# Low parts of every second down-projection block by a negated copy and an accumulating DMA

## The chip, the core and the metric

One core of a Trainium2 chip. Its engines work beside each other and meet at semaphores: PE (TensorE, matrix products), DVE (VectorE), ACT (ScalarE), POOL (GpSimd), and SP (SyncE), which here only issues DMAs. Each engine takes its instructions in the order of the program. The metric is the device time of one execution in microseconds (us), the median of several runs. The profile comes from one execution of its own.

## The reference

A decoder trunk of two layers over 256 tokens of width 1024. Each layer has three sub-layers: a SwiGLU with inner width 2816, a mixer (a gated recurrence, a state-space block and a gated token mixing, between two projections), and another SwiGLU. Around each stands a norm before and one after.

```
def swiglu(x, w_gu, w_down):
    g, u = jnp.split(x @ w_gu, 2, axis=-1)
    return (jax.nn.silu(g) * u) @ w_down

for l in range(DEPTH):
    f = swiglu(rms_norm(x, ffn1_pre_g[l]), ffn1_w_gu[l], ffn1_w_down[l])
    x = x + 0.5 * rms_norm(f, ffn1_post_g[l])
    m = hybrid_mixer(rms_norm(x, mix_pre_g[l]), mix_w_in[l], mix_w_out[l], ...)
    x = x + rms_norm(m, mix_post_g[l])
    f = swiglu(rms_norm(x, ffn2_pre_g[l]), ffn2_w_gu[l], ffn2_w_down[l])
    x = x + 0.5 * rms_norm(f, ffn2_post_g[l])
```

Everything is float32. The kernel reaches that precision with a faster product type (fp32r) by splitting each operand in a high part, its rounding to fp32r, and a low part, what the rounding left; three products (high by high, high by low, low by high) replace one.

## The kernel before

**Weights.** All weights stream through the core once, in the order of use, as blocks of 128 rows by 512 columns (some are narrower). Four blocks make a chunk. SyncE loads chunk after chunk (L345) into three staging buffers `stg` in turn, so chunk n + 3 goes into the buffer of chunk n as soon as all four blocks of chunk n have been read. A block is then split into a slot: a tile with a high half `hi` and a low half `lo`. There are 17 slots `s_w`, and a few spare ones (`s_a`) may be lent from another pool during a down projection. A slot comes free when PE has done the last product with its block. So weights are split ahead of PE as far as free slots reach.

**The split** (`split_next`, L383 to L404). Blocks that carry a norm's gain are scaled on the way (L400 on ScalarE, L401 on VectorE). Down-projection blocks carry none: ScalarE casts staging to the high half (L396), VectorE subtracts it from the staging for the low half (L397):

```
if not sc:
    self.keep(nc.scalar.copy(hi, src))
    self.keep(nc.vector.tensor_tensor(out=lo, in0=src, in1=hi.bitcast(F32), op=ALU.subtract))
```

**A SwiGLU** has six stages of gate and up products (L704), whose results go through silu, product and split on ScalarE and VectorE, and then the down projection (`down`, L738): 22 rows of two blocks, each block multiplied for two token tiles of 128, three products each (`mm3`, L425). The last four rows are done first for token tile 0 and then for token tile 1, so that the norm of tile 0 (`post`, L533) runs beside the products of tile 1. In `post`, ScalarE squares and sums each half of the result (tile `junk`), VectorE multiplies by the gain (`s_f`), POOL takes the power -1/2 (`postr`), VectorE makes the new x, and PE transposes it for the next sub-layer (`pre`, L569). These transposes stand in PE's order inside the products of tile 1.

**Order.** Python code issues side computations by planned times, and a scheduler then places the instructions of each engine. The result is one fixed list for each engine.

Of the kernel before, what the change touches and what calls it, by code (L numbers as in the profile page):

```python
# [8 lines left out]
F32 = mybir.dt.float32  # L9
F32R = mybir.dt.float32r  # L10
BF16 = mybir.dt.bfloat16
AF = mybir.ActivationFunctionType
# [3 lines left out]
P = 128  # L16
# [91 lines left out]


class Chain:  # L110
    """A side computation: a generator whose operations are issued when their inputs are due."""

    def __init__(self, k, t=None):
        self.k = k
# [107 lines left out]
class Kernel:  # L222
# [35 lines left out]
        self.wt, self.wh, self.wready, self.slot_time = {}, {}, {}, {}  # L258
        self.extra, self.keep_free = 0, 4

    # ---------------------------------------------------------------- memory
    def get(self, shape, dtype=F32, kind="a"):
        tag = self.free_slots[kind].pop(0)
        return self.scr.tile(shape, dtype, tag=tag, name="s_" + tag), (kind, tag)
# [24 lines left out]
        o, w = BCOL[name]  # L289
        return self.pb[:, o:o + w]  # L290

    # ---------------------------------------------------------------- issue order
    def keep(self, ins, pin=False):
        if pin or self.now() < PIN:
            self.tc.keep_in_program_order(ins)
# [39 lines left out]
    def drain(self):  # L335
        self.wait_for(lambda: not self.chains)

    # ---------------------------------------------------------------- weights
    def dma_chunk(self):
        ci = self.next_dma  # L340
        self.next_dma += 1
# [41 lines left out]
    def split_next(self, kind):  # L383
        d = self.next_split
        nc, T = self.nc, self.T
        u = self.units[d]
        w = unit_width(u)
        ci, o = self.u2c[d]
        src = self.ctile[ci][:, o:o + w]
        t, h = self.get([P, 2, 512], F32R, kind)  # L390
        hi, lo = t[:, 0, :w], t[:, 1, :w]
        sc = u[3] is not None
        T["act"] = max(T["act"], self.carrive[ci], self.slot_time.get(h, 0.0) + HOP) + 0.095 + w * 0.000833 + 0.095 * sc
        T["dve"] = max(T["dve"], T["act"] + HOP) + 0.07 + 0.06 * sc + w * 0.00104
        if not sc:
            self.keep(nc.scalar.copy(hi, src))  # L396
            self.keep(nc.vector.tensor_tensor(out=lo, in0=src, in1=hi.bitcast(F32), op=ALU.subtract))  # L397
        else:
            s = self.pcol(u[1], u[3][0], u[3][1])
            self.keep(nc.scalar.activation(hi, src, AF.Copy, scale=s))  # L400
            self.keep(nc.vector.scalar_tensor_tensor(out=lo, in0=src, scalar=s, in1=hi.bitcast(F32),  # L401
                                                     op0=ALU.mult, op1=ALU.subtract))
        self.wt[d], self.wh[d], self.wready[d] = t, h, T["dve"]
        self.next_split += 1  # L404
# [11 lines left out]
        self.slot_time[h] = self.now()  # L416
        self.put(h)

    # ---------------------------------------------------------------- main products
    def mm3(self, out, st, mv, start, stop):  # L420
        (sh, sl), (mh, ml) = st, mv
        mm = self.nc.tensor.matmul
# [11 lines left out]
        st = tuple(self.nT[:, i, k, t * P:(t + 1) * P] for i in range(2))  # L434
        self.mm3(bk[0][:, :w], st, (wt[:, 0, :w], wt[:, 1, :w]), start, stop)

    # ---------------------------------------------------------------- setup
    def setup(self):
        nc, cp = self.nc, self.cp
        self.cur = 0  # L440
# [21 lines left out]
        self.T["pool"] = 2.0  # L462

    def softplus(self, c, out, x, n, tag):
        """out = softplus(x) for [P, n] operands."""
        m, z, z2, p = (self.single([P, n], tag + s) for s in ("m", "z", "q", "p"))
        yield from c.stt(n, m, x, -1.0, x, ALU.mult, ALU.min)
        yield from c.act(n, m, m, AF.Exp, table="exp")
        yield from c.ts(n, z, m, 2.0, ALU.add)
        yield from c.op("dve", 0.15, self.nc.vector.reciprocal, z, z)  # L470
        yield from c.tt(n, z, m, z, ALU.mult)
        yield from c.tt(n, z2, z, z, ALU.mult)
        yield from c.ts(n, p, z2, 1.0 / 15, ALU.mult)
        for k in (13, 11, 9, 7, 5, 3):
            yield from c.stt(n, p, p, 1.0 / k, z2, ALU.add, ALU.mult)
        yield from c.stt(n, p, p, 1.0, z, ALU.add, ALU.mult)
        yield from c.ts(n, m, x, 0.0, ALU.max)
        yield from c.stt(n, out, p, 2.0, m, ALU.mult, ALU.add)
# [34 lines left out]
        self.keep(self.nc.scalar.dma_start(out=t, in_=self.gp_d[i:i + 1, :].partition_broadcast(P)), True)  # L513
        return t

    # ---------------------------------------------------------------- norms
    def rstd_of(self, c, ss, n, eps, name):
        v = self.small(1, name + "v")
        if n == 2:
# [11 lines left out]
        yield from c.act(n, self.junk()[:, :n], src, AF.Square, scale=scale, accum_out=out)  # L531

    def post(self, t, banks, gp, half, nxt):  # L533
        """x[t] += (0.5 if half else 1) * rms_norm(result, gp); then the next sub-layer's operand."""
        c = Chain(self)
        ev = self.ev[t]
        ss = self.small(2, "pss")
        fg, cs = [], []
        for n in range(2):
            yield from c.until(("acc", self.phase_of(nxt), t, n))  # L540
            a, v = c.fork(), c.fork()
            ps, tag, _ = banks[n]
            yield from self.square_sum(a, ps, 512, 1.0 / (16 if half else 32), ss[:, n:n + 1])
            f, h = yield from v.get([P, 512], F32, "f")
            yield from v.tt(512, f, ps, gp[:, n * 512:(n + 1) * 512], ALU.mult)
            fg.append((f, h))
            cs += [a, v]
            self.free_bank(tag, max(a.t, v.t))
        for i in (0, 2):
            c.join(cs[i])  # L550
        r = yield from self.rstd_of(c, ss, 2, ev if half else EPS, "post")
        c.join(*cs)
        xt = self.x[t]
        halves = []
        for n in range(2):
            sl = slice(n * 512, (n + 1) * 512)
            yield from c.stt(512, xt[:, sl], fg[n][0], r, xt[:, sl], ALU.mult, ALU.add)
            self.put(fg[n][1])
            if nxt == "out":
                self.nc.sync.dma_start(out=self.out_d[0, t * P:(t + 1) * P, sl], in_=xt[:, sl])  # L560
            else:
                halves.append(c.fork())
        if nxt != "out":
            yield from self.pre(t, nxt, halves)
# [2 lines left out]
        return self.cur_phase  # L567

    def pre(self, t, nxt, halves):  # L569
        """The operand of the next sub-layer, x transposed and split into two parts, and 1 / rms(x) by token.  # L570

        Products take x as it is; 1 / rms(x) goes to their results. A swiglu keeps it off u, and with it off
        the whole sub-layer's result, whose own norm then adds eps / rs^2 instead of eps.
        """
        kind, _, ph = nxt
        xt = self.x[t]
        for q in range(2):
            c = halves[q]
            ps, tag = yield from c.aux()
            for i in range(4):  # L580
                k = 4 * q + i
                yield from c.transpose(ps[:, i * P:(i + 1) * P], xt[:, k * P:(k + 1) * P])
            hi = self.nT[:, 0, 4 * q:4 * q + 4, t * P:(t + 1) * P]
            lo = self.nT[:, 1, 4 * q:4 * q + 4, t * P:(t + 1) * P]
            yield from c.split(512, hi, lo, ps.rearrange("p (k s) -> p k s", k=4))
            c.free_aux(tag)
            c.flag(("nT", ph, t, q))
        c = halves[1]
        c.t += 1.5
        ss = self.small(2, "prs")  # L590
        for n in range(2):
            yield from self.square_sum(c, xt[:, n * 512:(n + 1) * 512], 512, 1.0 / 32, ss[:, n:n + 1])
        v, r = (self.sp.tile([P, 1], F32, tag=f"{n}{t}", name=f"{n}{t}", bufs=2) for n in ("vx", "rs"))
        yield from c.stt(1, v, ss[:, 0:1], EPS, ss[:, 1:2], ALU.add, ALU.add)
        yield from c.op("pool", 0.47, self.nc.gpsimd.tensor_tensor, out=r, in0=v, in1=self.mhalf, op=ALU.pow)
        self.rs[t] = r
        c.flag(("rs", ph, t))
        if kind == "ffn":
            yield from c.ts(1, v, v, 4 * EPS, ALU.mult)
            self.ev[t] = v  # L600
        if t == 0:
            self.rb = self.sp.tile([P, SEQ], F32, tag="rb", name="rb", bufs=1)
        ps, tag = yield from c.aux()
        yield from c.mm(ps[:, :P], r.to_broadcast([P, P]), self.ident)
        yield from c.cast(P, self.rb[:, t * P:(t + 1) * P], ps[:, :P])
        c.free_aux(tag)
        c.flag(("rb", ph, t))

    # ---------------------------------------------------------------- ffn
    def evac_block(self, b, g, u, gtag, utag, t, width, hT, ph):  # L610
        c = Chain(self)
        sil, h1 = yield from c.get([P, 512], F32, "m")
# [77 lines left out]
        return self.down(lhs, d, gp, True, nxt)  # L690

    def b_tile(self, bk, half, d, col, last):
        """One 128-column tile of the product, features by tokens."""
        self.T["pe"] = max(self.T["pe"], bk[2] + HOP)
        for t in range(2):
            for q in range(2):
# [75 lines left out]
            self.put(*lhs[i][3])  # L772
        return d + 2 * n_k

    # ---------------------------------------------------------------- mixer
    def mixer(self, l, d, nxt):
        nc, ph = self.nc, self.phase
        gp = self.load_gpost(l * 3 + 1)
# [184 lines left out]
            c.flag(("mixT", ph, f, t))  # L963

    def decay(self, l):
        """dt, the decays within a chunk, exp(a_cs[l] - a_cs[s]) for s <= l, and the decays to its ends."""
        nc, M, ph = self.nc, self.M, self.phase
        c = Chain(self)
        d12 = lambda a: a.rearrange("p c h -> p (c h)")
# [91 lines left out]
        self.put(h_xdt, h_xd, M["zs_h"], M["bc_h"])  # L1061

    def scores(self, c, ch, bT, cT):
        """E[s, l] * (c[l] . b[s]) for s <= l, each head."""
        M, ph = self.M, self.phase
        e = M["E"][ch][0]
        ps, tag = yield from c.aux()
# [46 lines left out]
            yield from self.split_out(c, 3 + f, ch, ps[:, f * P:(f + 1) * P])  # L1114
        c.free_aux(tag)

    # ---------------------------------------------------------------- program
    def build(self):
        self.rs, self.ev = [None, None], [None, None]
        self.setup()  # L1120
# [78 lines left out]
```

## Time and profile before

| | us |
|---|---|
| median of three runs | 967.39 |
| lowest and highest run | 966.79, 967.49 |
| span of the profiled execution | 963.5 |
| PE busy in that span | 945.1 |
| VectorE busy | 649.1 |
| ScalarE busy | 580.4 |
| POOL busy | 40.1 |
| loads of 1 MB of weights | 147, at 5.0 from issue to landing |

The profile lists each engine's busy time, the groups of instructions by line and tile, what ended an engine's waits, and the chain of work that ended last, followed back from the end. A row such as `s_w<-stg` means that tile `s_w` is written from tile `stg`. The timelines give the start, the duration and, in brackets, how long the engine had stood and for whom. The granted clock of TensorE was 0.998 of full speed over the span.

### The profile page before, as it was taken

Reading aid. Unit: us, or ns where it says so; the run is one execution under the profiler, and the core shown is the slowest. Engines: PE = TensorE matmul, PEld = TensorE weight load, DVE = VectorE, ACT = ScalarE, POOL = GpSimd, SP = SyncE. Lnnn points to the kernel's source line nnn. Section 1 sums busy time; section 2 is a strip of 40 time slices with the busy share of each in tenths; the row PEclk is TensorE's granted clock in tenths of the full one; section 3 lists DMA queues with packets and bytes.
Section 4 is the critical chain, followed back from the end, with each engine's and each line's share of the span. In section 5 each row is a group of like instructions: output and inputs, shape, how many; then the busy total and the mean of one; then the engine's idle time right before and its main releaser. Section 6 shows DMA issues by size and latency. Waiting matters only on the chain.

```text
span 963.5 us, 16052 instructions
## 1 busy us (share of the span) xinstructions
PE 945.1 (98%) x6292; PEld 862.9 (90%) x6292; DVE 649.1 (67%) x1169; ACT 580.4 (60%) x1057; POOL 40.1 (4%) x58
## 2 busy tenths in 40 slices
PE   7999999999999999999999999999999999999997
PEld 6999998889986999998889999888999779999885
DVE  5876666566899856676565666666588996566632
ACT  7865555576967765555564555555589685454531
POOL 1100000001001100000010000000010110000000
PEclk9999999999999999999999999999999999999999
DMA  8855555443246945566435555663431566455621
GB/s 309 290 202 205 188 208 208 154 168 116 88 136 212 327 165 175 176 218 221 172 130 198 175 183 209 221 224 113 177 127 45 206 231 236 137 193 210 214 80 44
DMA packets 26717, 175.66 MB, mean 182 GB/s; under 512 B 2960, under 2 KB 3344, under 8 KB 7824
## 3 DMA queue, kind: packets, MB, share of 16 engines
q1 hardware_dynamic: 24768, 169.93, 50.0%
q10 hardware_dynamic: 1872, 4.70, 1.4%
q8 instruction: 49, 0.80, 0.3%
q14 instruction: 28, 0.23, 0.1%
HBM read 173.57 MB, written 1.05 MB: 181 GB/s over the span
## 4 chain that ended last, share of the span: by engine, by line
PE 89%; DVE 6%; ACT 2%; POOL 1%; issue 1%; DMA 0%; DVEq 0%; POOLq 0%; ACTq 0%
PE acc L704 46%; PE acc L425 39%; PE acc L137 4%; DVE s_w L401 2%; DVE s_a L137 1%; ACT s_a L137 1%; DVE x L137 1%; DVE s_f L137 1%; POOL postr L137 1%; DVE nT L137 1%; ACT L137 1%; POOL rs L137 0%; DMA x<-in_x_dram 0%; ACT junk L137 0%; POOL lnr L137 0%
## 5 line engine op out<-in xcount | busy, mean ns | idle before, releaser
L704 PE MATMUL acc<-nT,s_w 128*128 128x256 f32 x3900 | 467.5, 279 | 0.0
L704 PEld LDWEIGHTS acc<-nT,s_w 128*128 128x128 f32 x3900 | 460.3, 188 | 0.7
L401 DVE SCALAR_TENSOR_TENSOR s_w<-stg,pf,s_w 128x512 fp32r<-128x512 f32 (+2 forms) x435 | 299.2, 735 | 112.8 <-ACT s_w L400 112.5
L400 ACT ACTIVATE s_w<-stg,pf 128x512 fp32r<-128x512 f32 (+2 forms) x435 | 279.4, 701 | 113.7 <-PE acc L704 62.1
L425 PE MATMUL acc<-s_w,s_a 128*128 128x512 f32 x984 | 227.4, 390 | 0.0
L425 PEld LDWEIGHTS acc<-s_w,s_a 128*128 128x128 f32 x984 | 184.1, 188 | 37.9
L397 DVE TENSOR_TENSOR s_w<-stg,s_w 128x512 fp32r<-128x512 f32 x184 | 121.9, 687 | 61.9 <-ACT s_w L396 61.7
L396 ACT CAST s_w<-stg 128x512 fp32r<-128x512 f32 x184 | 107.0, 619 | 68.6 <-PE acc L425 36.7
L425 PE MATMUL acc<-s_w,nT 128*128 128x512 f32 (+1 forms) x522 | 129.3, 394 | 1.2 <-DVE nT L137 1.0
L425 PEld LDWEIGHTS acc<-s_w,nT 128*128 128x128 f32 x522 | 95.7, 189 | 21.6 <-DVE nT L137 2.3
L137 ACT ACTIVATE s_m<-s_m 128x512 f32<-128x512 f32 x36 | 22.6, 632 | 79.9 <-DVE s_m L137 79.9
L137 DVE TENSOR_TENSOR s_m<-acc,s_m 128x512 f32<-128x512 f32 (+1 forms) x64 | 35.7, 562 | 31.3 <-PE acc L704 25.8
L425 PE MATMUL acc<-s_w,s_m 128*128 128x512 f32 x192 | 48.0, 399 | 0.0
L425 PEld LDWEIGHTS acc<-s_w,s_m 128*128 128x128 f32 x192 | 34.8, 188 | 7.0 <-ACT s_m L137 0.5
L137 POOL TENSOR_TENSOR postr<-postv,mhalf 128x1 f32<-128x1 f32 x12 | 10.7, 893 | 705.7 <-DVE postv L137 705.7
L137 ACT CAST s_a<-s_m 128x512 fp32r<-128x512 f32 x36 | 22.1, 615 | 27.4 <-DVE s_m L137 26.9
L137 DVE TENSOR_TENSOR s_f<-acc,gp 128x512 f32<-128x512 f32 x24 | 16.5, 687 | 32.9 <-ACT junk L137 32.9
L137 ACT ACTIVATE junk<-acc 128x512 bf16<-128x512 f32 x24 | 14.2, 594 | 38.7 <-PE acc L425 38.2
L137 DVE TENSOR_TENSOR s_m<-acc,rb 128x512 f32<-128x512 f32 x36 | 24.7, 687 | 14.4 <-PE acc L704 14.4
L137 DVE TENSOR_TENSOR s_a<-s_m,s_a 128x512 fp32r<-128x512 f32 x36 | 24.7, 687 | 10.0 <-ACT s_a L137 10.0
L137 DVE SCALAR_TENSOR_TENSOR s_a<-s_f,pf,s_a 128x255 f32<-128x255 f32 (+2 forms) x60 | 28.5, 496 | 3.9 <-ACT s_a L137 3.9
L704 PE MATMUL acc<-nT,s_a 128*128 128x256 f32 x180 | 26.8, 279 | 0.0
(130 smaller groups left out, 526.0 us busy)
## 6 DMA issues: line engine op xcount, KB each, us to landing
stg<-in_wts_dram SPq DMA_DIRECT2D x147, 1024.0 KB, 5.0
stg<-in_wts_dram SPq DMA_DIRECT2D x12, 768.0 KB, 4.3
stg<-in_wts_dram SPq DMA_DIRECT2D x4, 780.0 KB, 4.4
gp<-in_gpost_dram ACTq DMA_DIRECT2D x6, 512.0 KB, 5.7
x<-in_x_dram SPq DMA_DIRECT2D x2, 512.0 KB, 4.4
out_dram<-x SPq DMA_DIRECT2D x4, 256.0 KB, 2.0
pb<-in_pb_dram ACTq DMA_DIRECT2D x2, 265.0 KB, 5.2
stg<-in_wts_dram SPq DMA_DIRECT2D x2, 256.0 KB, 4.6
```

The costliest lines, as they stand in the source:

```text
L137: ins = fn(*args, **kw)
L396: self.keep(nc.scalar.copy(hi, src))
L397: self.keep(nc.vector.tensor_tensor(out=lo, in0=src, in1=hi.bitcast(F32), op=ALU.subtract))
L400: self.keep(nc.scalar.activation(hi, src, AF.Copy, scale=s))
L401: self.keep(nc.vector.scalar_tensor_tensor(out=lo, in0=src, scalar=s, in1=hi.bitcast(F32), op0=ALU.mult, op1=ALU.subtract))
L425: self.keep(mm(out, a, b, start=start and i == 0, stop=stop and i == 2))
L704: self.keep(self.nc.tensor.matmul(out, a, b, start=k == 0 and i == 0, stop=k == KT - 1 and i == 2))
```

## The change

In every second block of a down projection (index `d` odd, 22 of 44 blocks in each of the four SwiGLUs) the low half is made in another way. ScalarE writes the negated high part into the low half (scale -1, the output type rounds), then the high half as before. POOL issues a DMA that reads the staged weights and adds them onto the low half. VectorE has no part in it. The planner's entry for VectorE's time is left as it was, ScalarE's gets one more copy, and the block counts as ready 3 us after that. The other lines of the diff take away comments and docstrings.

```
@@ split_next
         T["dve"] = max(T["dve"], T["act"] + HOP) + 0.07 + 0.06 * sc + w * 0.00104
+        if u[0].endswith("w_down") and d % 2:
+            T["act"] += 0.095 + w * 0.000833
+            self.keep(nc.scalar.activation(lo, src, AF.Copy, scale=-1.0))
+            self.keep(nc.scalar.copy(hi, src))
+            self.keep(nc.gpsimd.dma_start(out=lo.bitcast(F32), in_=src, accum_op=ALU.add))
+            self.wt[d], self.wh[d], self.wready[d] = t, h, T["act"] + 3.0
+            self.next_split += 1
+            return
         if not sc:
             self.keep(nc.scalar.copy(hi, src))
             self.keep(nc.vector.tensor_tensor(out=lo, in0=src, in1=hi.bitcast(F32), op=ALU.subtract))
```

PE's list is the same instruction for instruction, with the wait for a low half now on a DMA. The blocks of a down projection are called u0 to u43 here, those of the mixer that follows m0, m1 and so on.

ScalarE in the first down projection, before, from u28 to u35. `s_w14` is u28, `s_w15` u29, `s_w16` u30, `s_w0` u31, `s_w1` u32, `s_a11` u33, `s_w2` u34, `s_a12` u35; `stg_1700` holds u28 to u31, `stg_1726` u32 to u35:

```order
L396 CAST s_a11_1813<-stg_1726 128x512
L396 CAST s_a12_1825<-stg_1726 128x512
L396 CAST s_w14_1769<-stg_1700 128x512
L396 CAST s_w15_1778<-stg_1700 128x512
L396 CAST s_w16_1787<-stg_1700 128x512
L396 CAST s_w0_1796<-stg_1700 128x512
L396 CAST s_w1_1807<-stg_1726 128x512
L396 CAST s_w2_1819<-stg_1726 128x512
```

The same blocks after; `stg_1718` holds u28 to u31 and `stg_1748` u32 to u35, L397 is now the negated copy and L398 the high half of an odd block, L404 that of an even one:

```order
L404 CAST s_w14_1784<-stg_1718 128x512
L397 ACTIVATE s_w15_1792<-stg_1718 128x512
L398 CAST s_w15_1792<-stg_1718 128x512
L397 ACTIVATE s_a11_1829<-stg_1748 128x512
L404 CAST s_w16_1802<-stg_1718 128x512
L398 CAST s_a11_1829<-stg_1748 128x512
L397 ACTIVATE s_a12_1843<-stg_1748 128x512
L397 ACTIVATE s_w0_1811<-stg_1718 128x512
L398 CAST s_w0_1811<-stg_1718 128x512
L404 CAST s_w1_1823<-stg_1748 128x512
L398 CAST s_a12_1843<-stg_1748 128x512
L404 CAST s_w2_1836<-stg_1748 128x512
```

Before, both spare slots (u33, u35) were filled ahead of u28; after, they stand ahead of u30 and u31, and each odd block has two rows.

ScalarE at the end of that down projection, after. `stg_1815` holds u40 to u43, of which u43 went to `s_a0` and u41 to `s_w8`, both odd:

```order
L397 ACTIVATE s_a0_1916<-stg_1815 128x512
L404 CAST s_w7_1891<-stg_1815 128x512
L398 CAST s_a0_1916<-stg_1815 128x512
L397 ACTIVATE s_w8_1900<-stg_1815 128x512
L398 CAST s_w8_1900<-stg_1815 128x512
```

Further on, after, up to the square sums of token tile 0. `stg_1920` holds m8 to m11 (`s_w0` m8, `s_a2` m9, `s_w1` m10, `s_a3` m11), `stg_1883` m4 to m7 (`s_w15` m6, `s_w16` m7), `stg_2017` m20 to m23:

```order
L408 ACTIVATE s_a2_2002<-stg_1920,pf_79 128x512
L408 ACTIVATE s_a3_2014<-stg_1920,pf_79 128x512
L408 ACTIVATE s_w15_1975<-stg_1883,pf_79 128x390
L408 ACTIVATE s_w16_1984<-stg_1883,pf_79 128x390
L408 ACTIVATE s_w0_1995<-stg_1920,pf_79 128x512
L408 ACTIVATE s_w1_2008<-stg_1920,pf_79 128x512
L408 ACTIVATE s_w2_2027<-stg_1949,pf_79 128x512
L408 ACTIVATE s_a6_2256<-stg_2017,pf_79 128x384
L408 ACTIVATE s_a7_2269<-stg_2017,pf_79 128x384
L137 ACTIVATE junk_2048,pss_2036<-acc2_1637 128x512
L137 ACTIVATE junk_2064,pss_2036<-acc0_1639 128x512
```

From `s_w16` on the rows are those of before; `s_a2` has moved one place back, behind m5 (`s_w14`, the row above these).

SyncE's loads of two chunks in that projection, first of before, then of the change; the names in brackets are semaphores (DMAHW the loads' own, DMASW those of POOL's DMAs):

```order
L345 DMA stg<-in_wts_dram 128x2048 [waits DMAHW7_49,DVE_49]
L345 DMA stg<-in_wts_dram 128x2048 [waits DMAHW0_49,DVE_49]
```

```order
L345 DMA stg<-in_wts_dram 128x2048 [waits DMASW1_49,DMASW0_49,DMAHW7_49,DVE_49,Activation_49]
L345 DMA stg<-in_wts_dram 128x2048 [waits DMASW3_49,DMASW2_49,DMAHW0_49,DVE_49,Activation_49]
```

Each load now also waits for the two accumulating DMAs that read the buffer's former contents.

## The prediction

> **What bounds the kernel now.** I read the page's busy line first, then the chain that ended last, then the costliest groups.
>
> ```profile
> PE 945.1 (98%) x6292; PEld 862.9 (90%) x6292; DVE 649.1 (67%) x1169; ACT 580.4 (60%) x1057; POOL 40.1 (4%) x58
> ...
> PE 89%; DVE 6%; ACT 2%; POOL 1%; issue 1%; DMA 0%; DVEq 0%; POOLq 0%; ACTq 0%
> PE acc L704 46%; PE acc L425 39%; PE acc L137 4%; DVE s_w L401 2%; DVE s_a L137 1%; ACT s_a L137 1%; DVE x L137 1%; DVE s_f L137 1%; POOL postr L137 1%; DVE nT L137 1%; ACT L137 1%; POOL rs L137 0%; DMA x<-in_x_dram 0%; ACT junk L137 0%; POOL lnr L137 0%
> ...
> L397 DVE TENSOR_TENSOR s_w<-stg,s_w 128x512 fp32r<-128x512 f32 x184 | 121.9, 687 | 61.9 <-ACT s_w L396 61.7
> L396 ACT CAST s_w<-stg 128x512 fp32r<-128x512 f32 x184 | 107.0, 619 | 68.6 <-PE acc L425 36.7 <-DVE s_w L397 17.1 <-PE acc L704 14.8
> ```
>
> In the groups' rows the first number is busy time, the second the ns of one, then the idle time before and who ended it. PE is busy 98% of the span and carries 89% of the chain. L397, the subtraction that the change takes off VectorE in half of its blocks, is on the chain nowhere. So freeing VectorE pays nothing by itself, and what counts is whether something becomes late. Within a down projection PE never stands, and weights are ready far ahead of it:
>
> ```profile
> L397 DVE TENSOR_TENSOR s_w<-stg,s_w x184: 673/685/695, 115.3 to 930.2; 128x512 fp32r<-128x512 f32 x184
> ...
> L425 PE MATMUL acc<-s_w,s_a x984: 387/389/476, 134.5 to 955.6; 128*128 128x512 f32 x197
> ```
>
> The first down block is split at 115.3 and first multiplied at 134.5, a lead of 19 us.
>
> The places with no lead are the ends of sub-layers. First the chain (start, us, what) where the first sub-layer ends, with `postr` of the two others that matter, then PE's timeline there:
>
> ```profile
> 189.24 0.07 ACT junk L137
> ...
> 190.86 1.00 POOL postr L137
> ...
> 477.22 1.00 POOL postr L137
> ...
> 665.36 1.00 POOL postr L137
> ```
>
> ```profile
> 188.98 3.33 PE L425 MATMUL acc<-s_w,s_a 128*128 128x512 f32 x14
> 192.69 0.65 PE L137 MATMUL acc<-ident,x 128*128 128x128 f32 x4 [0.37 <-DVE x L137]
> ```
>
> ScalarE's square sum of the second half of token tile 0 (`junk`, 189.24) starts as soon as PE has finished that half. The norm and the new x follow, and PE, which works in order, waits at 192.69 for their transposes, with products of token tile 1 queued behind. This has no slack (PE already stood 0.37 us): **if ScalarE comes late to `junk`, PE stands as much longer.** It happens three times after a down projection that has a successor: at 190.86, again at 665.36 (474.50 later, the second layer's twin), and at 477.22.
>
> **The change, part by part.** I number a projection's blocks u0 to u43 (the odd ones change) and the mixer's first blocks m0 onward; four share a staging buffer.
>
> *Work moved.* 88 subtractions of 0.687 us leave VectorE: 60.5 us. ScalarE gains 88 copies at 0.619: 54.5 us. A pair of blocks then needs 3 x 0.62 = 1.9 us of ScalarE in the 2 x 1.36 us that PE takes for it (ScalarE rows 142.99 and 144.35 below), so throughput suffices. PE's cover for all of this is the 19 us lead. Direct cost: nothing. POOL gets 88 DMA issues; its `postr` stands behind 22 of them, but they go out with their blocks, long before 190.86.
>
> *A wait added on the staging buffers.* An odd block's staging is now read until its DMA has landed. SyncE, which reloads buffers in order, already waits for the last reader (238.0 us over 45 waits for L397). Its row of the waits, and the DMA issues with KB and us to landing:
>
> ```profile
> SPq L345 <- DVE s_w L397: 238.0, 45, 23.6
> ```
>
> ```profile
> stg<-in_wts_dram SPq DMA_DIRECT2D x147, 1024.0 KB, 5.0
> stg<-in_wts_dram SPq DMA_DIRECT2D x12, 768.0 KB, 4.3
> ...
> gp<-in_gpost_dram ACTq DMA_DIRECT2D x6, 512.0 KB, 5.7
> ...
> out_dram<-x SPq DMA_DIRECT2D x4, 256.0 KB, 2.0
> ...
> wst<-in_wst_dram ACTq DMA_DIRECT2D x2, 256.0 KB, 6.8
> ```
>
> ```profile
> L137 POOL TENSOR_TENSOR postr<-postv,mhalf 128x1 f32<-128x1 f32 x12 | 10.7, 893 | 705.7 <-DVE postv L137 705.7
> ```
>
> Let A be the time from the end of the negated copy to the landing of its DMA, and L = 5.0 a 1 MB load. No row shows an accumulating DMA. Below, 2.0: a 256 KB transfer with nothing beside it. Above, 6.8 + 0.9 = 7.7: 256 KB issued amid weight loads and other loads, plus the shortest POOL operation in the way of the issue. I take **A = 5.7**, the 512 KB row beside weight loads: the addition must fetch 256 KB of weights and 256 KB of low tile, also amid weight loads; I let POOL's issue time stand against this row's trip to HBM. So a buffer needs S = A + L = 10.7 us from its last odd copy to its next contents; before, 0.7 + 5.0.
>
> The Trainium skill's page "DMA: Bandwidth & Descriptors" (Anatomy of one DMA — SWDGE (gpsimd) path) fits 2.0 us plus bytes over 436 GB/s for a DMA issued by GpSimd: an estimate of 2.6 us for 256 KB, with which the sum below would be zero. The 512 KB row beside loads disagrees with such a fit (3.2 by it, 5.7 measured).
>
> Does S matter? ScalarE's rows, before:
>
> ```profile
> 132.33 4.27 ACT L396 CAST s_w<-stg 128x512 fp32r<-128x512 f32 x8 [1.85 <-PE acc L704]
> ...
> 142.99 0.62 ACT L396 CAST s_w<-stg 128x512 fp32r<-128x512 f32 x1 [0.74 <-PE acc L425]
> 144.35 0.62 ACT L396 CAST s_w<-stg 128x512 fp32r<-128x512 f32 x1 [0.74 <-PE acc L425]
> ...
> 150.62 1.14 ACT L396 CAST s_a<-stg 128x512 fp32r<-128x512 f32 x2 [0.21 <-DMA stg<-in_wts_dram]
> ...
> 161.41 0.62 ACT L396 CAST s_a<-stg 128x512 fp32r<-128x512 f32 x1 [0.17 <-DMA stg<-in_wts_dram]
> ...
> 173.90 0.72 ACT L400 ACTIVATE s_a<-stg,pf 128x512 fp32r<-128x512 f32 x1 [0.42 <-DMA stg<-in_wts_dram]
> ...
> 179.66 0.73 ACT L400 ACTIVATE s_w<-stg,pf 128x512 fp32r<-128x512 f32 x1 [0.63 <-PE acc L425]
> ...
> 185.67 1.12 ACT L400 ACTIVATE s_a<-stg,pf 128x384 fp32r<-128x384 f32 x2 [2.57 <-DMA stg<-in_wts_dram]
> 186.70 0.57 ACT L137 ACTIVATE junk<-acc 128x512 bf16<-128x512 f32 x1
> ...
> 189.24 0.60 ACT L137 ACTIVATE junk<-acc 128x512 bf16<-128x512 f32 x1 [1.87 <-PE acc L425]
> ...
> 420.06 4.27 ACT L396 CAST s_w<-stg 128x512 fp32r<-128x512 f32 x8 [1.84 <-PE acc L704]
> ...
> 475.60 0.60 ACT L137 ACTIVATE junk<-acc 128x512 bf16<-128x512 f32 x1 [2.77 <-PE acc L425]
> ```
>
> Most copies wait for PE to free a slot. The `s_a` copies do not: they fill spare slots **ahead of their turn**, read a buffer just landed, and ScalarE, in order, holds everything behind them. In the changed program u33 stands ahead of u30 and u31, u43 ahead of u40 and u41, m9 and m11 ahead of m6, m7, m8 and m10, and m20 and m22 ahead of `junk`. Each is loaded into the buffer of the group three earlier, and that buffer comes free with the very copies that were just held. So lateness is handed on, S each time. With 0.53 us a copy (4.27 over 8) and 0.62 for the scaled ones:
>
> - 132.33: PE frees the slots of u9 to u11. Four copies to the end of u11's negated one: 134.45.
> - + S: u20 to u23 have landed in that buffer. Five copies to u23's: + 2.67.
> - + S: u33's buffer is there. u33, u30, u33, u35, u31: + 2.67.
> - + S: u43's is there. u43, u40, u43, u41: + 2.14.
> - + S: m9's is there. Six copies to m10: + 3.6.
> - No accumulating DMA here: m10's low part on VectorE 0.8, a 768 KB load 4.3, two copies 1.1, the first `junk` 0.6.
>
> The second `junk` can start at 152.3 + 4 S; it is due at 189.24. The point from which it is late is S = 9.2, **A = 4.2**, and each us beyond costs four. With S = 10.7 it starts at 195.1: 5.9 us late. The blocks held up meanwhile, u30 to m10, come a few us later than before, well inside the lead of 19 us, so PE does not miss them. At u33, u35 and u31 three DMAs reach POOL within 2.7 us; at 0.9 each they go out as they come.
>
> At 477.22 the sum goes from 420.06, ends at the fourth buffer, then has six copies (3.8) and the first `junk` (0.6): 434.1 + 4 S = 476.9 against 475.60, 1.3 late. The last sub-layer has no successor.
>
> Sum: 2 x 5.9 + 1.3 = **13.1 us**. The profiled execution's span is 963.5, 3.9 under the median of the runs; its span would become 976.6, and the median 967.4 + 13.1 = **980.5**.
>
> **The rivals.**
>
> *The DMA is short, nothing is late.* With A up to 4.2 every wait above is hidden: 967.4. For it: 2.0 us for a 256 KB store alone, and a POOL that is 4% busy. The fit of the skill's page above gives this case. Against: one load of 5.0 us goes with every four blocks, 5.4 us of PE, so most of these DMAs run beside a load, and 5.7 and 6.8 are what transfers beside loads took. Chance 0.28.
>
> *The DMA is longer than 7.7.* If POOL takes long to issue, or the addition runs at a fraction of a copy's rate, say A = 9: S = 14, 2 x 19.1 + 14.5 = 53 us, 1020. It starts where A passes 7.7. For it: no row shows either cost. Against: every row of this size lies below. Chance 0.07.
>
> *VectorE's relief reaches the chain, faster.* Where a subtraction stands in front of the norm's operations on VectorE, taking it away would bring each of three sub-layer ends 0.69 us forward: 967.4 - 2.1 = 965.3. It needs a subtraction waiting there; in the order of VectorE the norm's rows have only the next sub-layer's blocks near them, and PE ends the wait of `junk` anyway. Chance 0.05.
>
> **How the numbers follow.** Forecast (A from 4.2 to 7.7): 0.60, likeliest 980.5, from 967.4 to 967.4 + 2 x 13.9 + 9.3 = 1004.5 (S = 12.7). Together with the first rival that is 0.88; the range is **966.5 to 1004.5**, its foot 0.9 under the median for scatter. About 0.2%, 1.9 us, is what a measurement of this kernel can tell from no change. Slower by more: 0.60 + 0.07 = 0.67; faster by more: 0.05; within: 0.28.
>
> **What would show it.** Right: accumulating DMAs landing 4.5 to 7.7 us after the copy; ScalarE's `s_a` copies waiting several us for `stg`; `junk` of token tile 0 late by the same amount at the ends of the first and fourth sub-layers, less at the third's, and PE standing there as long. Wrong, and then the time unchanged: landings under 4.2, or ScalarE at `junk` on time. Wrong in another way: PE standing inside a down projection for `s_w`, or a POOL busy all through it.

## The result and the profile after

| | median us | range us | runs |
|---|---|---|---|
| before | 967.24 | 966.79 to 967.49 | 4 |
| after | 1030.1 | 1027.46 to 1032.77 | 4 |

The ratio is 1.0654, 95% interval 1.0638 to 1.0671: **62.9 us slower**, where 13.1 was forecast. The profiled execution's span is 1029.7 against 963.5, 66.2 longer.

First the busy line and the engines' shares of the chain from the page of the changed kernel. Then, as `waiter <- releaser: us, times, longest`, three of its waits. Then its DMA issues with KB and median us to landing.

```profile
PE 960.2 (93%) x6292; PEld 870.7 (85%) x6292; DVE 594.7 (58%) x1081; ACT 616.9 (60%) x1145; POOL 116.4 (11%) x146
...
PE 57%; DMA 19%; DVE 8%; issue 7%; ACT 5%; POOL 3%; POOLq 0%; ACTq 0%; DVEq 0%; SPq 0%
```

```profile
SPq L345 <- DMA s_w<-stg: 268.5, 38, 13.3
```

```profile
ACT s_a L397 <- DMA stg<-in_wts_dram: 45.2, 8, 7.9
...
PE acc L137 <- DVE x L137: 41.1, 5, 16.7
```

```profile
stg<-in_wts_dram SPq DMA_DIRECT2D x147, 1024.0 KB, 5.2
s_w<-stg POOLq DMA_DIRECT2D x76, 256.0 KB, 6.5
...
s_a<-stg POOLq DMA_DIRECT2D x12, 256.0 KB, 6.1
```

VectorE lost 54.4 us of work and ScalarE gained 36.5; the run without the DMA below shows that neither matters. What matters is that DMA, 0% of the chain before, is 19% of it. SyncE waits for accumulating DMAs, ScalarE for loads, and PE stands at the transposes of the new x. The median load looks almost unchanged (5.2 for 5.0), but it is taken over the whole program. In the 55 us of the first down projection it reads otherwise; window rows (window, length, PE, PEld, DVE, ACT, POOL busy, granted clock, DMA share, GB/s), each with the issues of the same 55 us, first of before, then of after, there with its two queues (packets, MB, share of 16 engines):

```profile
137.00:192.00 55.00, 55.00 (x245) 45.46 (x243) 32.01 (x51) 29.08 (x51) 0.99 (x1) 1.00 0.58 207
```

```profile
stg<-in_wts_dram SPq DMA_DIRECT2D x7, 1024.0 KB, 4.9
```

```profile
137.00:192.00 55.00, 52.03 (x226) 42.01 (x226) 13.32 (x21) 27.97 (x54) 13.94 (x16) 1.00 0.96 245
```

```profile
q1 hardware_dynamic: 1296, 8.94, 49.0%
q0 software_dynamic: 2486, 4.50, 47.2%
...
stg<-in_wts_dram SPq DMA_DIRECT2D x6, 1024.0 KB, 7.5
s_w<-stg POOLq DMA_DIRECT2D x13, 256.0 KB, 6.7
```

The DMA engines go from 58% busy to 96%, and a load beside the additions takes 7.5 us, not 4.9. The chain of waits of the changed kernel (start, us, what) and ScalarE's timeline show the first sub-layer's end being made late, step by step:

```profile
143.89 8.20 DMA stg<-in_wts_dram
...
155.20 4.36 DMA s_w<-stg
159.71 9.85 DMA stg<-in_wts_dram
...
172.62 7.17 DMA s_w<-stg
...
179.93 6.26 DMA stg<-in_wts_dram
...
188.70 3.67 DMA s_w<-stg
192.50 5.97 DMA stg<-in_wts_dram
...
203.09 5.79 DMA stg<-in_wts_dram
...
212.26 1.01 POOL postr L137
```

```profile
135.03 0.63 ACT L397 ACTIVATE s_w<-stg 128x512 fp32r<-128x512 f32 x1
...
152.19 0.62 ACT L404 CAST s_w<-stg 128x512 fp32r<-128x512 f32 x1 [6.22 <-PE acc L433]
...
154.28 0.63 ACT L397 ACTIVATE s_w<-stg 128x512 fp32r<-128x512 f32 x1
...
169.58 0.63 ACT L397 ACTIVATE s_a<-stg 128x512 fp32r<-128x512 f32 x1 [3.79 <-DMA stg<-in_wts_dram]
...
171.68 0.61 ACT L397 ACTIVATE s_w<-stg 128x512 fp32r<-128x512 f32 x1
...
186.21 0.63 ACT L397 ACTIVATE s_a<-stg 128x512 fp32r<-128x512 f32 x1 [6.89 <-DMA stg<-in_wts_dram]
...
187.78 0.63 ACT L397 ACTIVATE s_w<-stg 128x512 fp32r<-128x512 f32 x1
...
198.50 1.33 ACT L408 ACTIVATE s_a<-stg,pf 128x512 fp32r<-128x512 f32 x2 [5.98 <-DMA stg<-in_wts_dram]
...
208.91 1.12 ACT L408 ACTIVATE s_a<-stg,pf 128x384 fp32r<-128x384 f32 x2 [6.21 <-DMA stg<-in_wts_dram]
...
210.63 0.60 ACT L137 ACTIVATE junk<-acc 128x512 bf16<-128x512 f32 x1
```

Read the two together: the negated copy of u11 ends at 135.66; its DMA goes out at 135.95, takes 7.8 us to land and lets SyncE load at 143.89; u20 is copied at 152.19. Then u23 (154.91), load 159.71, u33 at 169.58; u31 (172.29), load 179.93, u43 at 186.21; u41 (188.41), load 192.50, m9 at 198.50. ScalarE's 6.22 us before 152.19 are put down to PE, but the chain shows the load that landed just then. The second `junk` starts at 210.63, where it started at 189.24, and PE stands (PE's timeline of the changed kernel at the ends of sub-layers 1, 3 and 4):

```profile
214.10 1.12 PE L137 MATMUL acc<-ident,x 128*128 128x128 f32 x4 [16.71 <-DVE x L137]
...
515.61 1.11 PE L137 MATMUL acc<-ident,x 128*128 128x128 f32 x4 [6.84 <-DVE x L137]
...
724.88 1.11 PE L137 MATMUL acc<-ident,x 128*128 128x128 f32 x4 [15.86 <-DVE x L137]
```

PE runs the same instructions in the same order in both programs, so its lateness can be taken matmul by matmul from the two timelines (us that the changed kernel falls further behind):

| where | forecast | in the products before the stand | at the stand | after it | sum |
|---|---|---|---|---|---|
| at 36 us, before any changed block | 0 | | | | 1.1 |
| end of sub-layer 1 | 5.9 | 4.0 | 16.3 | 1.7 | 22.0 |
| end of sub-layer 3 | 1.3 | 7.0 | 6.5 | 2.7 | 16.2 |
| end of sub-layer 4 | 5.9 | 2.9 | 15.5 | 2.2 | 20.6 |
| last sub-layer | 0 | | | | 4.7 |
| everywhere else, with the end | 0 | | | | 1.6 |

Within the mixers and the first products of each SwiGLU nothing is lost.

### The profile page after: what moved, and what is told of

It is laid out like the page before. It is cut to its first block, busy times and chain, and to the rows that moved or that the text cites. A ratio compares the mean times of both kernels' runs of the same rounds, so it can differ in the third digit from the quotient of the medians.

```text
span 1029.7 us, 16385 instructions
## 1 busy us (share of the span) xinstructions
PE 960.2 (93%) x6292; PEld 870.7 (85%) x6292; DVE 594.7 (58%) x1081; ACT 616.9 (60%) x1145; POOL 116.4 (11%) x146
## 3 DMA queue, kind: packets, MB, share of 16 engines
q1 hardware_dynamic: 24768, 169.93, 47.9%
## 4 chain that ended last, share of the span: by engine, by line
PE 57%; DMA 19%; DVE 8%; issue 7%; ACT 5%; POOL 3%; POOLq 0%; ACTq 0%; DVEq 0%; SPq 0%
PE acc L712 36%; PE acc L433 16%; DMA stg<-in_wts_dram 13%; DMA s_w<-stg 6%; PE acc L137 4%; DVE s_w L409 3%; DVE s_a L137 2%; DVE s_f L137 1%; ACT s_a L137 1%; DVE x L137 1%; POOL s_w L399 1%; POOL postr L137 1%; ACT s_w L397 1%; DVE s_a L409 1%; ACT s_w L404 1%
## 5 line engine op out<-in xcount | busy, mean ns | idle before, releaser
L433 PE MATMUL acc<-s_w,s_a 128*128 128x512 f32 x984 | 238.9, 400 | 10.0 <-ACT s_w L404 6.3
L433 PEld LDWEIGHTS acc<-s_w,s_a 128*128 128x128 f32 x984 | 188.6, 193 | 54.4 <-ACT s_w L404 8.9
L405 DVE TENSOR_TENSOR s_w<-stg,s_w 128x512 fp32r<-128x512 f32 x108 | 74.3, 690 | 190.5 <-ACT s_w L404 182.7
L399 POOL DMA_DIRECT2D s_w<-stg x76 | 67.0, 882 | 520.4 <-ACT s_w L397 464.3
L404 ACT CAST s_w<-stg 128x512 fp32r<-128x512 f32 x108 | 65.1, 614 | 57.9 <-DMA stg<-in_wts_dram 39.8
L137 PE MATMUL acc<-ident,x 128*128 128x128 f32 x96 | 19.2, 339 | 45.9 <-DVE x L137 41.1
L137 PEld LDWEIGHTS acc<-ident,x 128*128 128x128 f32 x96 | 14.2, 174 | 51.2 <-DVE x L137 41.4
L397 ACT ACTIVATE s_w<-stg 128x512 fp32r<-128x512 f32 x76 | 47.7, 627 | 14.8 <-PE acc L712 14.8
L398 ACT CAST s_w<-stg 128x512 fp32r<-128x512 f32 x76 | 46.0, 605 | 0.0
L409 DVE SCALAR_TENSOR_TENSOR s_a<-stg,pf,s_a 128x512 fp32r<-128x512 f32 (+2 forms) x25 | 16.8, 716 | 33.0 <-ACT s_a L408 33.0
L397 ACT ACTIVATE s_a<-stg 128x512 fp32r<-128x512 f32 x12 | 7.6, 630 | 45.2 <-DMA stg<-in_wts_dram 45.2
```

The lines of the kernel that those rows point to most:

```text
L137: ins = fn(*args, **kw)
L397: self.keep(nc.scalar.activation(lo, src, AF.Copy, scale=-1.0))
L399: self.keep(nc.gpsimd.dma_start(out=lo.bitcast(F32), in_=src, accum_op=ALU.add))
L433: self.keep(mm(out, a, b, start=start and i == 0, stop=stop and i == 2))
```

## The experiments

Three theories went in. **H**: a buffer is held until its DMA lands, then reloaded, and ScalarE's copies ahead of their turn hand the lateness on: 4 (S − 9.2), S = hold + load. **E**: the 16 DMA engines themselves cannot keep PE's pace. **C**: ScalarE's second copy is too much. The addition's price for E comes from the queue rows below; a group of four blocks needs 2 x 1.51 of additions and 3.04 of a load (47.9% of 1029.7 us for 169.93 MB) = 6.1 us of all 16 engines, and PE takes 5.4 for it (4 x 1.36).

| run | median us | ratio, 95% interval | loss us |
|---|---|---|---|
| act_no_dma | 967.46 | 1.0004 (0.9994 to 1.0013) | 0.5 |
| bytes_no_hold | 996.60 | 1.0314 (1.0288 to 1.0341) | 29.6 |
| quarter_dma | 987.03 | 1.0201 (1.0180 to 1.0221) | 20.1 |
| plain_copy | 1000.24 | 1.0343 (1.0308 to 1.0379) | 33.3 |
| copy_no_hold | 978.46 | 1.0124 (1.0109 to 1.0140) | 11.9 |
| nstg4_slot15 | 1007.00 | 1.0420 (1.0405 to 1.0436) | 40.6 |
| slot15 | 1036.62 | 1.0717 (1.0691 to 1.0744) | 70.2 |
| early_pair | 1039.10 | 1.0762 (1.0715 to 1.0809) | 72.7 |
| no_spare | 1004.66 | 1.0388 (1.0371 to 1.0406) | 38.2 |
| one_in_four | 989.66 | 1.0247 (1.0232 to 1.0263) | 23.1 |
| quarter_nstg4 | 973.36 | 1.0075 (1.0060 to 1.0090) | 6.8 |
| quarter_no_spare | 971.80 | 1.0063 (1.0046 to 1.0080) | 5.2 |
| bytes_no_hold_no_spare | 975.57 | 1.0098 (1.0076 to 1.0120) | 8.5 |
| before_no_spare | 970.08 | 1.0033 (1.0020 to 1.0046) | 3.0 |
| before_nstg4_slot15 | 969.46 | 1.0032 (1.0018 to 1.0045) | 2.4 |

The loss is against the kernel before, run beside each (966.4 to 967.0).

**ScalarE's copies alone (act_no_dma).**

```diff
-            self.keep(nc.gpsimd.dma_start(out=lo.bitcast(F32), in_=src, accum_op=ALU.add))
+            self.keep(nc.vector.tensor_tensor(out=lo, in0=src, in1=lo.bitcast(F32), op=ALU.add))
```

> Odd down blocks: ScalarE still writes the negated copy, but VectorE adds the staging onto it and no DMA runs. Theory H (buffers are held until the DMA lands, each pass late by 4 (S - 9.2), S = hold + load): the hold is 0.7 us again, S about 5.7, nothing late, 966 to 969 us. Theory E (the DMA engines are full): no added bytes, also 966 to 969. Theory C (the second copy per block is too much for an in-order ScalarE): it stays near 1030.

0.5 us, and the interval holds no change. C falls: all 88 extra copies stand in ScalarE's order and cost nothing that shows. The whole loss comes with the DMA.

**The bytes without the hold (bytes_no_hold).**

```diff
-            self.keep(nc.gpsimd.dma_start(out=lo.bitcast(F32), in_=src, accum_op=ALU.add))
+            self.keep(nc.vector.tensor_tensor(out=lo, in0=src, in1=hi.bitcast(F32), op=ALU.subtract))
+            self.keep(nc.gpsimd.dma_start(out=lo.bitcast(F32), in_=hi.bitcast(F32), accum_op=ALU.add))
```

> VectorE makes the low part from the staging as before, and the accumulating DMA, equally large and equally many, then reads the high part in the slot, so no staging buffer waits for it; the low part comes out with the high part added, which no time depends on. H: the hold is about 1.4 us; loads still take about 7 us beside the DMAs, S about 8.5, under 9.2: 967 to 976 us. E (16 DMA engines need 6.1 us for four blocks that PE does in 5.4): at least 1010, since the engines' work is the same. C: near 1030.

29.6 us, between the two branches. Its first down projection (window row and issues), and one of its waits:

```profile
137.00:192.00 55.00, 54.46 (x240) 44.58 (x239) 27.81 (x45) 31.50 (x59) 14.34 (x17) 1.00 0.98 270
```

```profile
stg<-in_wts_dram SPq DMA_DIRECT2D x7, 1024.0 KB, 8.5
s_w<-s_w POOLq DMA_DIRECT2D x14, 256.0 KB, 13.3
```

```profile
ACT s_a L397 <- DMA stg<-in_wts_dram: 42.0, 8, 6.6
```

No buffer waits for an addition, yet loads take 8.5 us, and ScalarE's copies ahead of their turn wait for them as in the changed kernel. That alone is nearly half of the loss. A rival is that PE waits for the low parts themselves, which land late here. It does not hold: 20.2 us of PE's lateness arise at the transposes of the three ends, and PE's waits for these DMAs sum to under 3 us.

**The hold with few bytes (quarter_dma).**

```diff
-            self.keep(nc.gpsimd.dma_start(out=lo.bitcast(F32), in_=src, accum_op=ALU.add))
+            self.keep(nc.vector.tensor_tensor(out=lo[:96], in0=src[:96], in1=lo[:96].bitcast(F32), op=ALU.add))
+            self.keep(nc.gpsimd.dma_start(out=lo[96:].bitcast(F32), in_=src[96:], accum_op=ALU.add))
```

> The DMA adds only 32 of the 128 partitions (64 KB), VectorE the other 96; the staging is still held until the DMA lands. H with A and L stretched by the bytes: landing 3 to 4 us after the issue, loads 5.0 to 5.5, S about 9: 966 to 972 us. H with A a fixed cost of a DMA that GpSimd issues: landing still about 6, S about 11.3, 2 x 8.4 + 3.7: about 988 us. E: 966 to 972.

```profile
stg<-in_wts_dram SPq DMA_DIRECT2D x8, 1024.0 KB, 5.6
s_w<-stg POOLq DMA_DIRECT2D x14, 64.0 KB, 4.6
```

That is the same window. A quarter of the bytes shortens the landing to 4.6 us and the load to 5.6, and the loss falls by two thirds. The time came out where the other branch put it, but not by its mechanism: the landing isn't a fixed 6 us. With S = 0.1 + 4.6 + 5.6 = 10.3 (0.1 from ScalarE to GpSimd) the sum gives 4.4 at the first end; 6.9 were lost at its transposes, with the last load before the norm at 6.74 us in this run's chain where the sum has 4.3.

**A copy for the addition, with and without the hold (plain_copy, copy_no_hold).** The DMA lines are those of the changed kernel and of bytes_no_hold, without `accum_op`; the low half then holds the weight itself, or the high half.

> The same DMA without the addition: it copies the staging over the low part, so the low part is the weight itself. If the addition costs the DMA engines about twice a copy of the same bytes (1.6 us of all 16 engines now, a load 0.73 per 256 KB): landing about 4.5, loads about 6, S about 10.5, 2 x 5.2 + 0.5 = 11 us: 978, between 970 and 990. If reading and writing SBUF costs the same without the addition: 1020 to 1032.

> As the run in which the DMA reads the high part and holds no staging (996.6), but copying instead of adding, so the low part is the high part. E: a copy takes the DMA engines 0.68 us where an addition takes 1.5, loads are near 6 us for 8.2, S about 7.5, under 9.2: 967 to 975 us. If the bytes or the number of DMAs count and not the engines' time: 988 to 1000.

The queues (packets, MB, share of 16 engines; q1 carries the loads, q0 GpSimd's DMAs) over the whole span of the changed kernel, then q0 of plain_copy:

```profile
q1 hardware_dynamic: 24768, 169.93, 47.9%
q0 software_dynamic: 12672, 23.07, 12.9%
```

```profile
q0 software_dynamic: 7040, 23.07, 6.0%
```

88 DMAs take 0.129 x 1029.7 / 88 = 1.51 us of all 16 engines each as additions, 0.060 x 994.0 / 88 = 0.68 as copies: **an addition costs the engines 2.2 times a copy of the same bytes.** With the copy, loads in the window take 6.3 us with the hold and 6.8 without, and the losses fall from 62.9 to 33.3 and from 29.6 to 11.9. So the bytes alone do not set the loss: the same bytes as copies cost about half of it. The engines' time per DMA is the main difference; a smaller one is that GpSimd is held 0.33 us less to issue a copy, and the runs do not part the two. Both runs still lose more than expected (1000.2 for 970 to 990, 978.5 for 967 to 975).

**More buffers (nstg4_slot15), and its controls (slot15, before_nstg4_slot15).** `NSTG = 4` and `NSLOT = 15`.

> The changed kernel with four staging buffers, and 15 slots for 17 so that they fit. H (a buffer is held A and reloaded in L, and ScalarE hands the lateness on from one buffer's contents to the next): a buffer now serves every fourth group, three holds lie between the first blocks and the norm instead of four, 152 + 3 x 14 = 194 against 189: late by about 5 where it was 20; 975 to 990 us. E (16 DMA engines cannot carry loads and additions at PE's pace, buffers are beside the point): no better than 1020.

> The control of the run with four buffers: the changed kernel with 15 slots and still three buffers. H: the chain of four holds is unchanged, 1025 to 1045 us, a little worse since PE has two blocks less in stock. If slots are what counts and not buffers: over 1045.

> The kernel before with four staging buffers and 15 slots. If buffers cost it nothing: 966 to 970 us, with two slots less hardly felt; if the slots count: 971 to 975, and the 973.4 of the quarter DMA with these edits is all the edit's own.

A fourth buffer brings 1036.6 to 1007.0, so the hold counts; both controls came within their ranges. But 975 to 990 is missed: with more loads under way the engines are 99% busy in the same window, for 93% in slot15, and an addition takes 7.4 us to land, for 6.1; loads take 7.4, for 8.3. H alone is too simple; relieving the hold brings more loads beside the additions.

With quarter DMAs as well (quarter_nstg4, expected at 966 to 973) 6.8 us are lost, 2.4 of which the buffers and slots cost the kernel before. PE's stands at the transposes of the three ends are gone.

**The changed blocks first in their buffer (early_pair), and half as many (one_in_four).** `d % 2` becomes `d % 4 < 2` and `d % 4 == 1`.

> As many blocks are changed, but the first two of each four instead of the second and the fourth: the same bytes by DMA. H: the last DMA of a buffer goes out two copies earlier, S is 1.2 to 1.9 us shorter, 4 x 1.5 = 6 us less at each of three ends and some of the waits inside: 1005 to 1018 us. E: the same 1030.

> Only the second block of each four is changed: half the DMAs, and each goes out two copies before its buffer's last. H with E: the engines need 4.4 us for four blocks that PE does in 5.4, loads about 5.7, A about 5 less the two copies, S about 9: 967 to 982 us. If every DMA costs the same by itself: half of the loss, 998.

Both miss H's numbers. In early_pair PE's timeline shows why:

```profile
198.57 6.20 PE L433 MATMUL acc<-s_w,s_a 128*128 128x512 f32 x14 [6.45 <-DMA s_w<-stg]
...
220.06 1.12 PE L137 MATMUL acc<-ident,x 128*128 128x128 f32 x4 [11.87 <-DVE x L137]
```

The stand at the transposes shrinks from 16.7 to 11.9, as H says. But the block that is needed first out of a late buffer is now one whose low part comes by DMA, and PE stands for it inside the projection, 21.0 us in all for such blocks against 2.4 in the changed kernel. one_in_four loses 23.1 where 0 to 15 were expected: loads in the window take 6.1 us with 7 + 1 additions, not 5.7.

**No copies ahead of their turn (no_spare, quarter_no_spare, bytes_no_hold_no_spare, before_no_spare).** `EXTRA = 0`, in four kernels.

> The changed kernel without the six spare slots in the down projections: ScalarE's copies stand in PE's order and none reads a buffer ahead of its turn. H: at PE's pace a buffer's next contents are due 9 blocks, 12.2 us, after its last copy; with S of 14 it is 2 us late each time instead of 5, two to three times over: 975 to 995 us. If copies ahead of their turn don't hand anything on: 1030 or more, since six blocks less are in stock.

> The DMA adds 32 partitions and VectorE 96, three buffers, and no spare slots in the down projections. H: the hold of some 10 us fits into the 12.2 us that the buffers have at PE's pace, so nothing is handed on: 966 to 976 us, against 987 with spare slots. If spare slots are a help here as stock, not the way lateness travels: 990 or more.

> The accumulating DMA reads the high part and holds no staging buffer (996.6 with spare slots), and ScalarE has no spare slots in the down projections. H: loads stay near 8 us, but with 12.2 us from a buffer's last copy to its next contents' turn nothing is late: 967 to 977 us. E (the engines' throughput itself): 990 or more.

> The kernel before without the six spare slots in the down projections. If they are of little use there, as the lead of 17 blocks suggests: 966 to 971 us. If they carry the kernel over the norm: 972 or more, and that much of the runs without them is the edit's own.

The edit itself costs the kernel before 3.0 us. Against that, the short hold loses 2.2 (20.1 with spare slots), and the bytes without the hold 5.5 (29.6 with them). The latter's window:

```profile
137.00:192.00 55.00, 54.06 (x236) 43.62 (x235) 28.91 (x45) 33.56 (x61) 14.79 (x17) 1.00 0.99 285
```

```profile
stg<-in_wts_dram SPq DMA_DIRECT2D x8, 1024.0 KB, 8.1
```

The engines are 99% busy, loads take 8.1 us, and almost nothing is late. So E falls as a cause by itself; by an estimate from the figures above, 11 groups x 0.6 us = 7 us of work too much in a down projection, which fits into PE's lead of 19. Each part of the loss, taken alone, travels by the copies that ScalarE does ahead of their turn. With hold and bytes together (no_spare) 35 us remain over the edit's 3, and the 975 to 995 expected is missed by 10: a landing of 7.3 and a load of 8.8, the medians of the same window, are over the 12.2 that the buffers have at PE's pace.

None of these versions beats the kernel before.

## Why the prediction was wrong in size

**The step that failed: "L = 5.0 a 1 MB load" in S = A + L.** I priced the addition as one more transfer amid the loads and left the loads as they had been without it. The four links of the chain, from the rows of ScalarE and the chain above (end of the last negated copy to the next load, load to the first copy):

| link | hold | load |
|---|---|---|
| u11 to u20 | 8.23 | 8.30 |
| u23 to u33 | 4.80 | 9.87 |
| u31 to u43 | 7.64 | 6.28 |
| u41 to m9 | 4.09 | 6.00 |
| mean | 6.2 | 7.6 |
| forecast | 5.7 | 5.0 |

S was 13.8, not 10.7. With 13.8 for all four links at all three ends, the prediction's own sum gives 2 x 18.3 + 13.7 = 50 us, where the three ends lost 58.8. Of the 14.3 us by which the chain outgrew the forecast's (74.97 from 135.66 to 210.63, against 60.65), the loads of the four links are 10.4, the holds 2.0, and the last load before the norm, 5.79 for 4.3, 1.5. The chain also began 1.2 us late, about the 1.1 from 36 us. So A was good to 0.5 us on the mean of the four links; L was not. The chain itself, which copy hands on to which, ran as it was written down, link for link.

Why L grew is shown by the runs, not only argued: loads in the first down projection take 4.9 us in act_no_dma (engines 61% busy), 5.6 beside quarters (75%), and with nothing held 6.8 beside copies (78%) and 8.5 beside additions (98%), in the order of what the DMAs take of the engines. The Trainium skill's page "DMA: Bandwidth & Descriptors" (Issuing engines are not separate DMA queues) says that DMAs started by ScalarE, SyncE or GpSimd run on the same 16 engines and interleave; the trace agrees, with 49.0% of the engines' time in that window for the loads' queue and 47.2% for GpSimd's. No row of before had the price of an addition. But the 58% could be read there, and so could longer loads. The row that gave the bound of 6.8 us, `wst`, comes from places where transfers crowd. At the second of them the kernel before shows (window row and issue):

```profile
312.00:324.00 12.00, 12.00 (x67) 10.21 (x66) 10.27 (x16) 8.81 (x15) 3.17 (x3) 1.00 0.93 354
```

```profile
stg<-in_wts_dram SPq DMA_DIRECT2D x4, 1024.0 KB, 7.2
```

There the engines are 93% busy and a 1 MB load takes 7.2 us. The prediction took A from rows of transfers amid loads, and L from the median of the whole program.

Point by point:

- *Direct cost nothing, ScalarE's throughput suffices*: right (act_no_dma, +0.5).
- *The buffers' hold, handed on four times, ends in `junk`*: right in kind. For the 13.1 of the sum the stands measured 38.3.
- *"PE does not miss them"*: wrong. In the products before the stands PE lost 4.0, 7.0 and 2.9 us. With S at 13.8 some blocks came later than their lead of 19 us covers.
- *"The last sub-layer has no successor"*: wrong as a reason for no cost. PE waited inside that projection for late blocks (stands of 0.93, 0.23, 0.62 and 0.23 us between 1006 and 1009) and the rest came after them: 4.7 us.
- *The clock, not in the sum*: after each stand PE's products run slower for some us. The windows after the first and third ends in the changed kernel, granted clock 0.72 and 0.73 (1.00 in the window of before that follows its first end, 192 to 200), and the products' row with min/median/max ns:

```profile
212.00:222.00 10.00, 7.90 (x35) 7.14 (x36) 7.55 (x15) 7.29 (x16) 1.86 (x2) 0.72 0.19 55
...
515.00:527.00 12.00, 11.39 (x43) 9.40 (x44) 10.03 (x18) 6.43 (x16) 1.98 (x2) 0.73 0.58 196
```

```profile
L433 PE MATMUL acc<-s_w,s_a x984: 387/389/797, 135.7 to 1020.4; 128*128 128x512 f32 x197
```

  It adds 1.7 to 2.7 us to each stand, 6.6 in all. The Trainium skill's page "TensorE: Matmul & The Clock Gate" (Part 1: The HAM clock gate) has the clock halved after a window of idleness; the longest product here, 797 ns against a median of 389 (476 at most before), agrees.
- *Rival: the DMA is short, nothing late*: fell. Landings were 3.3 to 11.3 us, median 6.2. The estimate of 2.6 us from the Trainium skill's page "DMA: Bandwidth & Descriptors" (Anatomy of one DMA — SWDGE (gpsimd) path), which it drew on, is below the shortest addition here and near the shortest copy, 2.3. The 512 KB row with which the prediction set it aside was issued by ScalarE, so it did not test a DMA of GpSimd.
- *Rival: the DMA longer than 7.7*: gave a time of the right order, 1020, by a cause that the chain does not show: the mean hold of its four links was 6.2. The nearness of the number is luck. (The bound of 7.7 took `postr`, 0.9 us, for the shortest POOL operation; `lnr` takes 0.55, which would put it near 7.3.)
- *Rival: VectorE's relief*: VectorE was relieved by 54 us in a kernel that got slower. act_no_dma, without the relief, and the kernel before are alike, so nothing shows such a gain.

Still open: the 1.1 us at 36 us stand ahead of any changed block and come in some of the runs and not in others; their cause was not looked for. And the hold was never measured at full bytes with loads of their old length: relieving one changed the other, so no split of the 62.9 us between them is shown.

## What to carry to other kernels

Before moving an engine's work to a DMA, read the DMA engines' share in the stage it moves to, and add the engines' time of the new transfers to it. The other transfers of that stage grow longer too, and they did so well before the engines were full: in the first down projections of these runs loads took 4.9 us at 58 to 61% busy, 5.5 to 6.8 at 75 to 79%, and 7.4 to 8.8 at 85 to 99%. A price per transfer is not enough; the loads that were there before were the larger term. And where an in-order engine reads buffers ahead of their turn, a delay in refilling is passed on once per refill: taking away the read-ahead took away most of the loss that either part caused alone.

## What the runs showed of the hardware that was not expected

- An accumulating DMA from SBUF to SBUF (256 KB) takes 1.51 us of all 16 DMA engines, a copy 0.68; a 64 KB addition 0.49 (4.4% of 985.9 us over 88). GpSimd's queue counts 144 packets for an addition and 80 for a copy.
- Where no buffer waited for the additions, one took far longer to land than any row had hinted: a median of 13.3 us in bytes_no_hold's first down projection, 18.6 at most. The busy share alone does not set this: in nstg4_slot15, with the engines 99% busy too, it was 7.4. In those 55 us up to seven additions were on the way at once in bytes_no_hold, up to five in nstg4_slot15. SyncE's loads beside them were stretched less, 4.9 to 8.5.
- Issuing one held GpSimd for 0.862 us, a copy for 0.536 (medians).
